# Latent attention: four of nine key tiles with one fp32 tile of exponentials and one plain fp32 value product

## The chip, the core and the metric

The kernel runs on one core of a Trainium2 chip. The core has a matrix engine (TensorE, PE in the profile, with its weight loads shown apart as PEld), a vector engine (VectorE, DVE), a scalar engine with the exponential (ScalarE, ACT), a general engine (GpSimd, POOL) and a sync engine that issues the DMAs (SyncE, SP). Each engine works through its own list of instructions in order and waits on semaphores for the others. The metric is the time of one execution on the device in microseconds; lower is better.

## The reference

Two layers of a diffusion trunk are computed in fp32 for 128 context tokens and 1024 latent tokens. Layer 0 joins a banded attention and a bidirectional state-space scan. Layer 1, which the change concerns, is a multi-head latent attention of 16 heads:

```python
def dense_attention(q, k, v, scale, sink=None):
    ...
    def one_block(qblk):
        s = jnp.einsum("bqhgd,bkhd->bhgqk", qblk, k).astype(jnp.float32) * scale
        ...
            p = jax.nn.softmax(s, axis=-1)
        return jnp.einsum("bhgqk,bkhd->bqhgd", p.astype(v.dtype), v)
...
    k = jnp.concatenate([k_lat, k_ctx], axis=1)
    v = jnp.concatenate([v_lat, v_ctx], axis=1)
    return mla_attend(q, k, v, g, w_out)
```

For every head the 1024 latent queries see 1024 latent keys and 128 keys of the cached context (nine key tiles of 128); the 128 new context tokens see only themselves (one key tile). Keys and queries have 96 columns, values 64.

## The kernel before

float32r is a type that the matrix engine reads at a reduced precision in one pass. To stay near fp32, the kernel splits nearly every operand into two float32r parts, high and low, whose sum is the fp32 value (`split`, L245: ACT rounds the high part, DVE or POOL subtracts for the low one), and multiplies three pairs of parts (`mm3`, L255). A few products run as plain fp32: the scan's state product (L992), the sums of the softmax (L1496) and some small ones.

Layer 1's attention is woven from generators. `head_main` (L1437) is the main stream. For each head it goes over three chunks of queries: 512 and 512 latent ones with nine key tiles each, and the 128 context ones with one. A step for one key tile does this:

- Three score products into one of two PSUM banks (L1449 to L1451). The row of minus the maximum is a 97th row of the operands, so that the exponential needs no further subtraction.
- Two exponentials from the same scores on ACT: `ph` as float32r (L1458) and `pf` as fp32 (L1459).
- One step later, in `rest`, DVE computes the low part `pl` = `pf` - `ph` (L1473) and POOL adds `pf` to the chunk's running denominators, `total` (L1477; L1475 for the single-tile chunk).
- Behind that, in `values`, two products with the values add into the chunk's bank `acco` (L1467 with `ph`, L1468 with `pl`). Their stationary operand is a tile of 128 keys by 128 columns: 64 columns with the high part of the values, 64 with the low part.

`gather` (L1484) adds both halves of the chunk's outputs (L1489, L1490), sums `total` over its partitions by a plain product with ones (L1496), and later divides and gates. The rings are short: three buffers for `pf` and `ph`, two for `pl`, two for `total`, two banks for scores.

Beside the main stream run the row maxima of the next heads (`head_max`: PE L1428, then a DVE reduction that the profile shows at L209, since its call is put off by `Steps.tick`), the projections of the next pair of heads (`operands`, with PE at L256 to L258 and splits at L249 and L250), and at the end the splitting of the output weights. `spread` (L1548) deals these evenly over the main steps. A scheduler of the tile framework then fixes the order on every engine from its own model of durations, so an edit in one place can move instructions of others.

Of the kernel before, what the change touches and what calls it, by code (L numbers as in the profile page):

```python
# [80 lines left out]
class Segment:  # L81
    """columns of one SBUF tile, handed out and taken back while the kernel is traced"""

# [26 lines left out]
class Memory:  # L110
    """four tiles of SBUF: R holds operands of float32r products, F everything else, S and G either by turns"""

# [25 lines left out]
class Space:  # L138
    """named rings of buffers in the memory"""

# [52 lines left out]
class Steps:  # L193
    """pieces of work put off by a number of steps of the stream that they go along with"""

# [25 lines left out]
def hybrid_trunk(ctx: ExitStack, tc: tile.TileContext, I, O, dbg=None, stage=99):  # L221
# [23 lines left out]
    def split(hi, lo, src, scale=None, lo_eng=None):  # L245
        """hi + lo == src * scale exactly; scale is None, a power of two or a [P, 1] operand."""
        lo_eng = lo_eng or dve
        if scale is None:
            act.copy(hi, src)  # L249
            lo_eng.tensor_tensor(lo, src, hi.bitcast(F32), ALU.subtract)  # L250
        else:
            act.activation(hi, src, AF.Copy if isinstance(scale, float) else AF.Identity, scale=scale)  # L252
            dve.scalar_tensor_tensor(lo, src, scale, hi.bitcast(F32), ALU.mult, ALU.subtract)
# [5 lines left out]

# [1 line left out]
    ident = const("ident", [128, 128], I["k_ident"])  # L261
# [8 lines left out]

# [1 line left out]
    gate_d = scratch("gate_d", [2, 2, D])  # L272
# [20 lines left out]

# [1 line left out]
    wp = Space(mem)  # L295
# [19 lines left out]

# [1 line left out]
    def condition():  # L317
# [25 lines left out]
    def modulation(sp, l, j, parts):  # L343
        """columns 256 j .. 256 j + 255 of the map of layer l; whole weights, or split ones where TensorE has no time to spare"""
        c0 = j * 256
# [42 lines left out]
    def rstd_of(p, ssq, n, width):  # L388
        """ssq [128, width] -> (ssq / n + eps) ** -0.5"""
        r = p.tile([128, width], F32, tag="rstd", name="rstd", bufs=4)  # L390
        pool.tensor_scalar(r, ssq, 1.0 / n, EPS, ALU.mult, ALU.add)
        pool.tensor_tensor(r, r, minus_half, ALU.pow)
        return r
# [7 lines left out]
    def weave(main, n_main, aux, n_aux):  # L401
        """n_aux steps of aux spread evenly over n_main steps of main"""
        done = 0
        for i, _ in enumerate(main):
            while done < n_aux and done * n_main < n_aux * (i + 1):
                next(aux, None)
                done += 1
        for _ in aux:
            pass

    def token_tile(hT, t):
        """the transposes of token tile t, by k: two parts"""
        c, o = divmod(t, CH // 128)
        return [h[:, :, o * 128:(o + 1) * 128] for h in hT[c]]
# [3 lines left out]

# [1 line left out]
    condition()  # L420
# [35 lines left out]

# [1 line left out]
    wp.drop("wr")  # L458
# [242 lines left out]

# [1 line left out]
    def fm_proj(w, b, hT, c):  # L703
        """128 columns of a slab for a chunk of tokens, columns by tokens"""
        acc = psum("mm", "acc")
        ws = slice(b * 128, (b + 1) * 128)
        for k in range(KT):
            mm3(acc[:, 0:CH], w[0][:, k, ws], w[1][:, k, ws], hT[c][0][:, k], hT[c][1][:, k], k == 0, k == KT - 1)
        return acc[:, 0:CH]
# [61 lines left out]
    def chunk_states(p, fb, xt, Bt):  # L771
        """states of two heads before every chunk, forward ones at rows 0..63, backward ones, counted from the last chunk, below"""
        g, h0 = slice(fb // 4 * 64, fb // 4 * 64 + 64), 2 * fb
# [146 lines left out]

# [1 line left out]
    mem.set("G", F32)  # L922
# [119 lines left out]

# [1 line left out]
    def norm_T(p, l, cond, xh, tok):  # L1044
        """modulated transpose of a normalised token tile"""
        for q in range(2):
# [9 lines left out]
    def residual(p, half, acc, x, gate, adder=pool):  # L1056
        """x[:, half] += gate * acc"""
        cs = slice(half * 512, (half + 1) * 512)
        tmp = p.tile([128, 512], F32, tag="rt", name="rt", bufs=2)
        dve.tensor_tensor(tmp, acc, gate[:, cs], ALU.mult)  # L1060
        adder.tensor_tensor(x[:, cs], x[:, cs], tmp, ALU.add)
# [90 lines left out]

# [1 line left out]
    mem.set("G", F32R)  # L1154
# [11 lines left out]
    with p6 as p:  # L1166
        order = [NLT] + list(range(NLT))

        def put_latent(tk, n):
            """tk [128, n * 128 + 96]: transposes of the columns of cq, ckv and (at rows 64..95) kpe"""  # L1170
            pt = psum("tr", "pt")
            for j in range(n):
                pe.transpose(pt[:, j * 128:(j + 1) * 128], tk[:, j * 128:(j + 1) * 128], ident)
            pe.transpose(pt[0:32, 384:512], tk[:, n * 128:n * 128 + 32], ident)
            return pt
# [71 lines left out]

# [1 line left out]
    uq = I["mla_w_uq"][0].rearrange("(k p) (h d) -> p k h d", p=128, d=96)  # L1249
# [20 lines left out]
    def pinned(f, *a):  # L1270
        """an instruction that stays behind those that its engine was given before"""
        tc.keep_in_program_order(f(*a))  # L1272
# [3 lines left out]
    def spare(name):  # L1276
        """a bank, to be read in the next step"""
        taken.append(steps.now)
        assert taken.count(steps.now) <= 4
        return psum(next(either), name)  # L1280
# [3 lines left out]
    def until(n):  # L1284
        """waits for the n-th step from now"""
        t = steps.now + n
# [48 lines left out]
    def quad_rope(Q):  # L1335
        """the rotated parts of four heads' queries"""
        qh, ql = quads[Q][0]
# [30 lines left out]
    def place(Q, pr, acc, dh, dl, cols):  # L1368
        """a pair of heads' rows of a projection into their operand sets"""
        for a in range(2):  # L1370
# [16 lines left out]
    def operands(pair):  # L1387
        """fills the operand sets of a pair of heads"""
        Q, pr = divmod(pair, 2)
# [10 lines left out]
    def head_max(h):  # L1400
        """row of -max of the scores, a group of query tiles at a time"""
        s = h % NSET
# [19 lines left out]
        for t0, n in ((0, 4), (4, 4), (NLT, 1)):  # L1422
            pm = p7.tile([128, 4, 3], F32, tag="pm", name="pm", bufs=3)
            spans = [(NL + 128, 128)] if t0 == NLT else [(c * CH, CH) for c in range(3)]
            for t in range(t0, t0 + n):
                for c, (k0, w) in enumerate(spans):
# [5 lines left out]
                    yield  # L1432

    CHUNKS = ((0, 512, range(9)), (512, 512, range(9)), (NL, 128, (9,)))
    behind = []

    def head_main(h, op, chunks=CHUNKS):  # L1437
        """a step per tile of keys: its scores and exponentials; the values of the tile before"""
        s, a = h % NSET, h % 2
        for q0, n, kts in chunks:  # L1440
# [5 lines left out]
            for i, kt in enumerate(kts):  # L1446
# [8 lines left out]
                pf = p7.tile([128, 512], F32, tag="pf", name="pf", bufs=3)[:, 0:n]  # L1455
                ph = p7.tile([128, 512], F32R, tag="ph", name="ph", bufs=3)[:, 0:n]
                pl = p7.tile([128, 512], F32R, tag="pl", name="pl", bufs=2)[:, 0:n]
                act.activation(ph, sc[:, 0:n], AF.Exp, scale=SCALE_M)  # L1458
                act.activation(pf, sc[:, 0:n], AF.Exp, scale=SCALE_M)  # L1459
# [3 lines left out]

                def values(V=quads[h // 4][2][h // 2 % 2][:, kt, a], ph=ph, pl=pl, acc=acc, total=total, i=i, last=i == len(kts) - 1, q0=q0, n=n):
                    if i == 0:
                        acc.append(psum("o", "acco")[:, 0:n])
                    pe.matmul(acc[0], V, ph, start=(i == 0), stop=False)  # L1467
                    pe.matmul(acc[0], V, pl, start=False, stop=last)  # L1468
                    if last:
                        after(1, gather, h, op, q0, n, acc[0], total)  # L1470

                def rest(pf=pf, ph=ph, pl=pl, total=total, i=i, alone=len(kts) == 1, first=first, values=values):
                    dve.tensor_tensor(pl, pf, ph.bitcast(F32), ALU.subtract)  # L1473
                    if alone:
# [9 lines left out]
    def gather(h, op, q0, n, acc, total):  # L1484
        """adds the two parts of a head's outputs; divides a pair of heads by the denominators, gates"""
        a, j = h % 2, h // 2
# [61 lines left out]
    def spread(n_main, *aux):  # L1548
        """called once a step of n_main: steps of every (generator, count) spread evenly"""
        done = [0] * len(aux)  # L1550
# [87 lines left out]

# [1 line left out]
    with p9 as p:  # L1640
# [59 lines left out]
```

## Time and profile before

| what | value |
|---|---|
| median of three runs | 1939.34 us (1937.37 to 1945.99) |
| span of the profiled execution | 1936.3 us |
| PE busy in it | 1770.5 us |
| DVE busy | 1338.3 us |
| ACT busy | 972.3 us |
| POOL busy | 849.1 us |
| granted TensorE clock, mean | 0.952 |
| from the first value product to the last sum of denominators | 1160 to 1836 us of the span |

The page gives no time of its own for the profiled execution beside its span; the median lies 3.0 us above it. Busy times are of single engines and overlap. In rows that group instructions, the part in front of the bar names line, engine, operation, output and inputs with their shapes and the count; behind it stand the busy time, the mean in ns of one, and the idle time in front with what ended it. A wait row names who waited, on whom, and total us, times and the longest. All SBUF tiles of this kernel are columns of four large tiles, so that names like arenaF say only which of the four; the line tells which work it is. A plain fp32 product appears as two instructions on PE.

### The profile page before, as it was taken

The page shows a single profiled execution, that of the slowest core. Times are in us where ns is not written, and L with a number is a line of the kernel's source. Part 1 is how long each engine was busy: PE and PEld are TensorE (multiplying, and loading weights), DVE is VectorE, ACT ScalarE, POOL GpSimd, SP SyncE. Part 2 cuts the span into 40 slices and gives each one's busy share as a digit, 9 for nine tenths or more (in the row PEclk, how much of TensorE's full clock was granted, in tenths as well). Part 3 has the DMA queues.
Part 4 walks back from the last instruction along what each step waited for, and adds up shares of the span by engine and source line. Part 5 has one row for each costly group of instructions (what it writes and reads, how often), then busy time and mean ns, then how long its engine had stood idle before and what let it go on. Part 6 is the DMA issues. An engine that isn't in the chain of part 4 may idle for free. (4 is left out here: it accounts for less than half of the span.)

```text
span 1936.3 us, 28171 instructions
## 1 busy us (share of the span) xinstructions
PE 1770.5 (91%) x9031; PEld 1405.9 (73%) x9031; DVE 1338.3 (69%) x2421; ACT 972.3 (50%) x2201; POOL 849.1 (44%) x781
## 2 busy tenths in 40 slices
PE   7899999999987898989999999998989899988898
PEld 3899999868766866767788986666666566654586
DVE  5666455654544577676654359999999899999833
ACT  5533224655654454444344236666567566765521
POOL 3410000233443346566340105866775586765632
PEclk9999999999988888989999989999989899998999
DMA  7333333343436786554535320211120121112352
GB/s 256 111 91 111 93 105 104 118 121 98 127 110 186 232 262 212 167 185 157 170 89 177 107 64 12 60 27 38 33 60 19 40 63 30 33 40 89 91 168 87
DMA packets 210664, 210.33 MB, mean 109 GB/s; under 512 B 36162, under 2 KB 175504, under 8 KB 210516
## 3 DMA queue, kind: packets, MB, share of 16 engines
q1 hardware_dynamic: 210372, 208.40, 35.7%
q8 instruction: 72, 1.18, 0.3%
q14 instruction: 76, 0.62, 0.1%
q0 software_dynamic: 144, 0.13, 0.0%
HBM read 151.94 MB, written 51.72 MB: 105 GB/s over the span
## 5 line engine op out<-in xcount | busy, mean ns | idle before, releaser
L1477 POOL TENSOR_TENSOR arenaF<-arenaF 128x512 f32<-128x512 f32 x256 | 390.9, 1528 | 171.4 <-PE den L1496 96.0
L256 PE MATMUL acc<-arenaR 128*128 128x384 f32 (+4 forms) x1152 | 390.6, 340 | 14.4 <-ACT arenaR L252 4.7
L257 PE MATMUL acc<-arenaR 128*128 128x384 f32 (+3 forms) x1080 | 362.7, 336 | 0.1
L258 PE MATMUL acc<-arenaR 128*128 128x384 f32 (+4 forms) x1056 | 352.1, 335 | 0.8 <-DVE arenaR L250 0.6
L256 PEld LDWEIGHTS acc<-arenaR 128*128 128x128 f32 x1152 | 224.3, 195 | 41.2 <-issue 7.0
L209 DVE TENSOR_REDUCE arenaF<-pp 128x1 f32<-128x384 f32 (+1 forms) x400 | 204.0, 534 | 21.6 <-PE pp L1428 18.9
L257 PEld LDWEIGHTS acc<-arenaR 128*128 128x128 f32 x1080 | 210.0, 194 | 10.7 <-issue 1.8
L258 PEld LDWEIGHTS acc<-arenaR 128*128 128x128 f32 x1056 | 206.0, 195 | 13.2 <-issue 3.0
L1473 DVE TENSOR_TENSOR arenaG<-arenaF,arenaS 128x512 fp32r<-128x512 f32 (+1 forms) x202 | 200.0, 996 | 3.9 <-PE acco L1468 2.7
L1459 ACT ACTIVATE arenaF<-sc 128x512 f32<-128x512 f32 (+1 forms) x304 | 174.3, 576 | 7.3 <-POOL arenaF L1477 6.7
L1468 PE MATMUL acco<-arenaG 128*128 128x512 f32 (+1 forms) x304 | 134.1, 444 | 42.9 <-DVE arenaG L1473 38.5
L1458 ACT ACTIVATE arenaS<-sc 128x512 fp32r<-128x512 f32 (+1 forms) x202 | 117.3, 582 | 91.0 <-PE sc L1451 46.1
L1005 ACT ACTIVATE arenaG<-arenaG,arenaF 128x128 f32<-128x128 f32 x288 | 88.4, 389 | 115.9 <-POOL arenaG L1003 115.4
L250 DVE TENSOR_TENSOR arenaR<-arenaF,arenaR 128x512 fp32r<-128x512 f32 (+2 forms) x135 | 115.3, 869 | 41.9 <-ACT arenaR L249 35.5
L249 ACT CAST arenaR<-arenaF 128x512 fp32r<-128x512 f32 (+3 forms) x151 | 91.6, 625 | 81.2 <-DMA arenaF<-in_ab_w_in_dram 19.1
L1468 PEld LDWEIGHTS acco<-arenaG 128*128 128x128 f32 x304 | 59.5, 196 | 98.7 <-DVE arenaG L1473 88.1
L258 PE MATMUL acc<-arenaR,arenaS 128*128 128x512 f32 (+1 forms) x336 | 128.9, 387 | 0.0
L749 POOL TENSOR_TENSOR arenaG<-arenaF,arenaG 128x512 fp32r<-128x512 f32 x28 | 48.6, 1734 | 151.4 <-PE acco L753 83.4
L1428 PE MATMUL pp<-arenaR 96*128 96x384 f32 x300 | 104.3, 385 | 8.4 <-DVE arenaF L209 4.2
L256 PE MATMUL acc<-arenaR,arenaS 128*128 128x512 f32 (+1 forms) x264 | 106.3, 403 | 1.0 <-ACT arenaS L249 0.7
L257 PE MATMUL acc<-arenaR,arenaS 128*128 128x512 f32 (+1 forms) x264 | 105.4, 399 | 0.0
L1449 PE MATMUL sc<-arenaR 96*128 96x512 f32 (+1 forms) x228 | 96.5, 423 | 7.1 <-ACT arenaF L1459 6.9
(339 smaller groups left out, 4052.9 us busy)
## 6 DMA issues: line engine op xcount, KB each, us to landing
arenaF<-in_ada_w_dram SPq DMA_DIRECT2D x96, 256.0 KB
arenaG<-cum_d SPq DMA_DIRECT2D x36, 512.0 KB
arenaF<-in_ab_w_in_dram SPq DMA_DIRECT2D x51, 256.0 KB
z_d<-arenaF SPq DMA_DIRECT2D x36, 128.0 KB
xs_d<-arenaF SPq DMA_DIRECT2D x8, 576.0 KB
arenaF<-xs_d SPq DMA_DIRECT2D x9, 512.0 KB
arenaF<-z_d SPq DMA_DIRECT2D x9, 512.0 KB
x_d<-arenaG SPq DMA_DIRECT2D x9, 512.0 KB
```

Source lines behind the costliest of these rows:

```text
L209: f()
L250: lo_eng.tensor_tensor(lo, src, hi.bitcast(F32), ALU.subtract)
L256: pe.matmul(out, ah, bh, start=first, stop=False)
L257: pe.matmul(out, ah, bl, start=False, stop=False)
L258: pe.matmul(out, al, bh, start=False, stop=last)
L1428: pe.matmul(pp[:, 0:w], AQ[s][0:96, t * 128:(t + 1) * 128], AK[s][0:96, k0:k0 + w], start=True, stop=True)
L1449: pe.matmul(sc[:, 0:n], AK[s][0:96, ks], BQ[s][:, qs], start=True, stop=False)
L1458: act.activation(ph, sc[:, 0:n], AF.Exp, scale=SCALE_M)
L1459: act.activation(pf, sc[:, 0:n], AF.Exp, scale=SCALE_M)
L1468: pe.matmul(acc[0], V, pl, start=False, stop=last)
L1473: dve.tensor_tensor(pl, pf, ph.bitcast(F32), ALU.subtract)
L1477: pool.tensor_tensor(total, first if i == 1 else total, pf, ALU.add)
```

## The change

Of the nine key tiles of a chunk, those with index 1, 3, 5 and 7, and the only tile of the context chunk, are called whole. For them `ph`, its exponential, `pl` and the subtraction are left out, and the values meet `pf` in one plain fp32 product; the stationary operand is the same tile, read as fp32. The other five key tiles stay as they were. Comments and docstrings are removed elsewhere in the file, and lines from L1434 on move down by one to eight.

```diff
+    WHOLE = 1, 3, 5, 7
...
-                ph = p7.tile([128, 512], F32R, tag="ph", name="ph", bufs=3)[:, 0:n]
-                pl = p7.tile([128, 512], F32R, tag="pl", name="pl", bufs=2)[:, 0:n]
-                act.activation(ph, sc[:, 0:n], AF.Exp, scale=SCALE_M)
+                whole = i in WHOLE or len(kts) == 1
+                ph = pl = None
+                if not whole:
+                    ph = p7.tile([128, 512], F32R, tag="ph", name="ph", bufs=3)[:, 0:n]
+                    pl = p7.tile([128, 512], F32R, tag="pl", name="pl", bufs=2)[:, 0:n]
+                    act.activation(ph, sc[:, 0:n], AF.Exp, scale=SCALE_M)
                 act.activation(pf, sc[:, 0:n], AF.Exp, scale=SCALE_M)
...
-                    pe.matmul(acc[0], V, ph, start=(i == 0), stop=False)
-                    pe.matmul(acc[0], V, pl, start=False, stop=last)
+                    if whole:
+                        pe.matmul(acc[0], V.bitcast(F32), pf, start=(i == 0), stop=last)
+                    else:
+                        pe.matmul(acc[0], V, ph, start=(i == 0), stop=False)
+                        pe.matmul(acc[0], V, pl, start=False, stop=last)
...
-                    dve.tensor_tensor(pl, pf, ph.bitcast(F32), ALU.subtract)
+                    if not whole:
+                        dve.tensor_tensor(pl, pf, ph.bitcast(F32), ALU.subtract)
```

In the kernel after, the scores are L1450 to L1452, the plain product L1472, the two parts L1474 and L1475, the subtraction L1481, the exponentials L1462 (`ph`) and L1463 (`pf`), the denominators' addition L1485 and their sum L1504.

PE's queue while the projections of the second pair of heads are made, from the last product of a key projection (L258) on. Before (a name in brackets is the semaphore for which the instruction waits):

```order
L258 MATMUL acc<-arenaR 128x256
L1449 MATMUL sc<-arenaR 128x512 [waits Activation_49]
L1450 MATMUL sc<-arenaR 128x512
L1451 MATMUL sc<-arenaR 128x512 [waits DMAHW2_49,DMAHW3_49,DMAHW1_49,DMAHW0_49]
L1428 MATMUL pp<-arenaR,arenaS 128x384 [waits DVE_49]
L1468 MATMUL acco<-arenaG 128x512 [waits DVE_49]
L1467 MATMUL acco<-arenaR,arenaG 128x512
L1449 MATMUL sc<-arenaR 128x512 [waits Activation_49]
```

The same place after:

```order
L258 MATMUL acc<-arenaR 128x256
L1475 MATMUL acco<-arenaG 128x512 [waits DVE_49]
L1472 MATMUL acco<-arenaF,arenaG 128x512
L1428 MATMUL pp<-arenaR,arenaS 128x384 [waits DVE_49,PE_49]
L1474 MATMUL acco<-arenaS,arenaG 128x512 [waits Activation_49]
L1428 MATMUL pp<-arenaR,arenaS 128x384 [waits DVE_49]
L1450 MATMUL sc<-arenaR 128x512 [waits Activation_49]
L1451 MATMUL sc<-arenaR 128x512
```

The plain product (L1472, its input `pf` in arenaF) stands directly behind the second part of the tile ahead of it (L1475), which waits for DVE, and the first part of the next tile (L1474) follows. That is so for 102 of the 144 plain products; before, the next tile's first part mostly stood in that place.

DVE's queue between the two splits of that key projection (L250, 64x256). Before:

```order
L250 TENSOR_TENSOR arenaR<-acc,arenaR 64x256 [waits Activation_49]
L209 TENSOR_REDUCE arenaF<-pp 128x1 [waits PE_49]
L1473 TENSOR_TENSOR arenaG<-arenaF,arenaS 128x512 [waits PE_49]
L209 TENSOR_REDUCE arenaF<-pp 128x1 [waits PE_49]
L1473 TENSOR_TENSOR arenaG<-arenaF,arenaS 128x512 [waits PE_49,Activation_49]
L250 TENSOR_TENSOR arenaR<-acc,arenaR 64x256 [waits Activation_49]
```

After, up to the next subtraction:

```order
L250 TENSOR_TENSOR arenaR<-acc,arenaR 64x256 [waits Activation_49]
L209 TENSOR_REDUCE arenaF<-pp 128x1 [waits PE_49] x2
L250 TENSOR_TENSOR arenaR<-acc,arenaR 64x256 [waits Activation_49]
L1407 TENSOR_REDUCE arenaF<-arenaF 128x4 [waits DVE_49]
L209 TENSOR_REDUCE arenaF<-pp 128x1 [waits PE_49]
L1408 TENSOR_SCALAR arenaF<-arenaF 128x4 [waits DVE_49]
L1481 TENSOR_TENSOR arenaG<-arenaF,arenaR 128x512 [waits Activation_49]
```

The two subtractions between the splits are gone, and the row maxima's reductions (L209) and the next ones' last steps (L1407, L1408) have moved up. POOL's queue keeps its additions, and SP's DMAs are nearly in the old order.

More of the change, by code (lines that the diff above doesn't have):

```diff
@@ L1462, in head_main, with values, rest @@
                     behind.pop()()
-                def values(V=quads[h // 4][2][h // 2 % 2][:, kt, a], ph=ph, pl=pl, acc=acc, total=total, i=i, last=i == len(kts) - 1, q0=q0, n=n):
+                def values(V=quads[h // 4][2][h // 2 % 2][:, kt, a], whole=whole, pf=pf, ph=ph, pl=pl, acc=acc, total=total, i=i, last=i == len(kts) - 1, q0=q0, n=n):
                     if i == 0:
                         acc.append(psum("o", "acco")[:, 0:n])
-                    pe.matmul(acc[0], V, ph, start=(i == 0), stop=False)
-                    pe.matmul(acc[0], V, pl, start=False, stop=last)
+                    if whole:
[3 more added lines that the diff above has]
+                        pe.matmul(acc[0], V, pl, start=False, stop=last)
                     if last:
                         after(1, gather, h, op, q0, n, acc[0], total)
-                def rest(pf=pf, ph=ph, pl=pl, total=total, i=i, alone=len(kts) == 1, first=first, values=values):
-                    dve.tensor_tensor(pl, pf, ph.bitcast(F32), ALU.subtract)
+                def rest(whole=whole, pf=pf, ph=ph, pl=pl, total=total, i=i, alone=len(kts) == 1, first=first, values=values):
+                    if not whole:
+                        dve.tensor_tensor(pl, pf, ph.bitcast(F32), ALU.subtract)
                     if alone:
```

## The prediction

> **What bounds the kernel now.** The first view is the table of stretches, cut where the attention's first value product starts and where its last denominator ends. Its columns are the stretch, its length, then busy time with the count of instructions for PE, PE's weight loads, DVE, ACT and POOL, then the granted clock, the DMA share and GB/s.
>
> ```profile
> 0.00:1160.00 1160.00, 1071.74 (x6184) 911.63 (x6185) 672.09 (x1289) 517.57 (x1243) 367.84 (x432) 0.95 0.47 144
> 1160.00:1836.00 676.00, 606.35 (x2444) 418.77 (x2444) 629.61 (x1093) 437.29 (x932) 449.61 (x313) 0.96 0.17 45
> 1836.00:1936.30 100.30, 92.44 (x405) 75.51 (x403) 36.56 (x40) 17.44 (x27) 31.69 (x36) 0.99 0.37 125
> ```
>
> The edited lines run only in the middle stretch of 676 us, and everything outside it stays. In it DVE is busy 630 us (93%), PE 606 us (90%), POOL 450 us (67%), ACT 437 us (65%). DMA is slight. PE's 90% flatters it, because each record contains the fill of the array. So the second view is the timeline of PE, to see how far apart matmuls start when nothing holds them: first a 512-wide float32r run, then a 384-wide one.
>
> ```profile
> 903.31 0.39 PE L256 MATMUL acc<-arenaR,arenaS 128*128 128x512 f32 x1
> 903.53 0.39 PE L257 MATMUL acc<-arenaR,arenaS 128*128 128x512 f32 x1
> 903.76 0.40 PE L258 MATMUL acc<-arenaR,arenaS 128*128 128x512 f32 x1
> ...
> 1207.56 0.34 PE L256 MATMUL acc<-arenaR 128*128 128x384 f32 x1
> 1207.74 0.34 PE L257 MATMUL acc<-arenaR 128*128 128x384 f32 x1
> ```
>
> A record lasts 0.39 us but the next starts after 0.22 to 0.24 us (I use 0.233, the middle of many such steps), and after 0.18 us at 384 columns. How much PE really has to do follows from the counts in the same stretch, one row for each output tile, here sc (scores), acco (values), pp (row maxima), acc (projections), den (denominators) and pt (transposes):
>
> ```profile
> 1160.00:1836.00 676.00, 270.57 (x906) 169.94 (x906) 318.82 (x606) 0.96 0.17 45
> 1160.00:1836.00 676.00, 207.28 (x608) 108.33 (x608) 25.55 (x47) 22.89 (x48) 0.96 0.17 45
> 1160.00:1836.00 676.00, 128.94 (x377) 72.58 (x377) 192.14 (x377) 0.96 0.17 45
> 1160.00:1836.00 676.00, 88.70 (x411) 71.36 (x410) 73.55 (x161) 56.51 (x143) 0.96 0.17 45
> 1160.00:1836.00 676.00, 39.92 (x95) 4.56 (x96) 21.38 (x47) 0.96 0.17 45
> 1160.00:1836.00 676.00, 14.10 (x47) 4.16 (x47) 0.00 (x0) 11.47 (x47) 0.96 0.17 45
> ```
>
> Scores and values: 858 + 576 wide ones by 0.233 = 334 us. pp: 361 by 0.18 = 65. acc: 411 of mixed width, about 0.175 each by the two steps above, 72. den: 32 wide by 0.95 and 16 narrow by 0.31 (rows below), 35. The 128-wide rest and the transposes, an estimate, 11. That is **517 us of real PE work**, so 159 us of the stage are PE waiting, loading weights in the open, or running at a lowered clock. The third view, the table of waits for this stretch, says on whom (us in total, times, longest):
>
> ```profile
> PEld acco L1468 <- DVE arenaG L1473: 88.1, 116, 2.5
> PE acco L1468 <- DVE arenaG L1473: 38.5, 65, 1.9
> PEld pp L1428 <- DVE arenaF L209: 22.8, 63, 1.4
> PEld sc L1449 <- ACT arenaF L1459: 20.0, 38, 1.4
> PEld den L1496 <- issue: 14.0, 41, 0.7
> PEld pp L1428 <- issue: 8.5, 19, 1.6
> PE sc L1449 <- ACT arenaF L1459: 7.6, 15, 1.2
> PEld pt L1413 <- DVE arenaF L1408: 7.5, 12, 3.0
> ```
>
> 126.6 of these 207 us (61%) are the value product waiting for DVE's subtraction at L1473. So DVE is the bound today, and it is exactly DVE that the change relieves; but PE, which the change loads, has only those 159 us to give.
>
> **The change part by part.** Four of nine key tiles in each of 32 chunks are 128 wide tiles; the 16 context chunks are 16 narrow ones. The groups by shape give what goes:
>
> ```profile
> L1473 DVE TENSOR_TENSOR arenaG<-arenaF,arenaS 128x512 fp32r<-128x512 f32 x192 | 197.1, 1032 | 3.9 <-PE acco L1468 2.7 <-ACT arenaF L1459 1.1
> L1473 DVE TENSOR_TENSOR arenaG<-arenaF,arenaR 128x512 fp32r<-128x512 f32 x96 | 98.4, 1025 | 1.8 <-PE acco L1468 1.4 <-ACT arenaF L1459 0.2
> L1458 ACT ACTIVATE arenaS<-sc 128x512 fp32r<-128x512 f32 x192 | 114.5, 598 | 88.1 <-PE sc L1451 44.7 <-DVE arenaG L1473 29.9 <-PE acco L1467 4.1
> ```
>
> DVE loses 128 x 1.03 = 132 us and about 5 us of narrow ones: 630 becomes 493 us, 73% of today's stage. ACT loses 128 x 0.598 = 77 us and about 4: 437 becomes 356 us, 53%. POOL's sums stay, 450 us. None of this is a gain by itself; it counts only as far as PE stops waiting.
>
> What PE gains: the plain product of a 128x128 stationary with 512 columns. The nearest rows of before are the plain fp32 products of the scan stage (64 rows, but also 128 stationary columns and 512 moving ones), and the denominators (one stationary column):
>
> ```profile
> 912.23 1.12 PE L992 MATMUL off<-arenaG,arenaF 64*128 64x512 f32 x2
> 913.28 0.50 PE L256 MATMUL acc<-arenaR 128*128 128x512 f32 x1
> 913.62 0.40 PE L257 MATMUL acc<-arenaR 128*128 128x512 f32 x1
> ...
> 918.62 0.39 PE L258 MATMUL acc<-arenaR 128*128 128x512 f32 x1
> 918.94 1.12 PE L992 MATMUL off<-arenaG,arenaF 64*128 64x512 f32 x2
> ...
> 1206.06 0.34 PE L258 MATMUL acc<-arenaR,arenaS 128*128 128x384 f32 x1
> 1206.33 1.02 PE L1496 MATMUL den<-arenaF 128*1 128x512 f32 x2
> 1207.27 0.45 PE L1428 MATMUL pp<-arenaR 96*128 96x384 f32 x1
> ...
> 1208.72 0.38 PE L1496 MATMUL den<-arenaF 128*1 128x128 f32 x2
> 1209.03 0.45 PE L1428 MATMUL pp<-arenaR 96*128 96x384 f32 x1
> ```
>
> One plain product is two records (x2). From its start to the next it takes 1.05 us (912.23 to 913.28), 0.94 us with a single stationary column. It starts 0.32 instead of 0.23 us behind its forerunner (918.62 to 918.94), and its follower's successor comes 0.34 instead of 0.23 us later (913.28 to 913.62). Together 1.05 + 0.09 + 0.11 = 1.25 us against 2 x 0.233 = 0.466 for the two parts: **+0.78 us a tile, 100 us for 128**. The low end is the denominators' 0.94 + 0.09 + 0.11 = 1.14 (+86 us); I take 1.25, since the stationary has 128 columns. A narrow one costs 0.31 + 0.2 against some 0.16: 16 x 0.35 = 6 us. PE's work becomes 517 + 106 = **623 us**.
>
> The Trainium skill, TensorE: Matmul & The Clock Gate, section "Step-by-step: what each phase is for", says that the next weights load while this matmul runs; FP8 and Floating Point Precision, section "TensorE Precision Notes", counts four passes for true fp32. By both a plain tile would take 4 x 0.233 = 0.93 us and the 128 tiles add 59 us, 41 us less than my sum. The trace agrees with the four passes and disagrees with the hiding: at each change between fp32 and float32r the rows above show about 0.1 us, and 0.1 more between the two records. I go by the rows.
>
> What is left of the 159 us decides. DVE's part is 61% of it, 97 us: 4/9 of those waits vanish, since a plain tile needs no subtraction, and the others shrink with DVE at 73%; I take a quarter, 25 us. The other 62 us (a lowered clock is some 27 of them, 0.04 x 676; the rest are waits for ACT and for reductions, and loads around the denominators) I take at half, 30 us, because ACT and DVE both have slack then. Stage: 623 + 55 = 678 us, 2 us over today. Bounds: at best only edges remain, 22 us, stage 645 (-31); at worst only 4/9 of 126.6 goes, 103 us remain, stage 726 (+50).
>
> Two edits have no direct price. The fp32 tile pf now stays in use until PE has read it, and its ring has three buffers; today's rows for such waits are small:
>
> ```profile
> ACT arenaF L1459 <- POOL arenaF L1477: 6.7, 14, 1.0
> ACT arenaS L1458 <- PE acco L1467: 4.6, 8, 1.2
> ```
>
> I take nothing, up to 10 us, covered by two steps between the exponential and the slot's reuse. The new order of PE's queue puts the plain product mostly right behind its neighbour's second part, which waits for DVE; behind it stand the next scores, for which ACT waits. That is the second rival.
>
> **The rivals.**
>
> *Faster: PE is kept fed.* PE reaches 95% of real work once DVE has slack, and its lowered clock goes with the gaps that cause it. For it speaks how the clock falls:
>
> ```profile
> 1408.00:1412.00 4.00, 2.35 (x7) 1.15 (x7) 2.66 (x10) 2.18 (x7) 3.58 (x3) 0.90 0.49 135
> 1412.00:1416.00 4.00, 4.00 (x13) 3.21 (x13) 2.00 (x4) 1.57 (x6) 3.03 (x3) 0.50 0.58 161
> ```
>
> PE busy for 2.35 of 4 us, then a granted clock of 0.50. If such gaps close, most of the 27 us return, 35 us of the 159 remain, the stage takes 658 us and the kernel 1936.3 - 18 + 3 = 1921 us. Against it: the stage would have PE with work for 95% of the time, in order, with two score banks. The Trainium skill's section "The HAM clock gate" in TensorE: Matmul & The Clock Gate states that an idle window of some 3.4 us halves the clock; these two rows agree in kind.
>
> *Slower: PE's queue is held.* PE is the bound and its in-order queue still stops at the second parts; the 1.25 us products then stand between a late subtraction and the scores, ACT runs dry, and every wait is now a wait of the bound. With 85 us remaining the stage takes 708 us, the kernel 1971 us. It decides from 53 us of remaining waits on (676 - 623). For it: 102 of the 144 plain products stand directly behind a second part in the new order. Against it: DVE at 73% should have finished that part earlier.
>
> That the change doesn't take effect has no chance: the order has 144 plain products and the subtractions fewer by as many.
>
> **How the numbers follow.** The span of the profiled execution is 1936.3 us; the median of the three runs, 1939.34, is 3.0 above, and I carry that over. Forecast: +2 us, **1941 us**, chance 0.36 for all within 0.5% (about what a measurement of this kernel can tell from no change), that is 43 to 63 us of remaining waits. The faster rival has 0.34, the slower one 0.30. The range reaches from the best bound, 1908 us, to near the worst, 1978 us; the forecast's own is 1930 to 1949 us.
>
> **What would show it.** Plain products start-to-start near 1.05 us with about 0.1 us on either side (0.93 without would make it 40 us faster). L1473's group at 160 instructions, DVE near 500 us, ACT near 356 us in the stage. The waits of PE for that line under 40 us if the forecast or the faster rival holds, over 60 if the slower one does. PE's chain share should grow at DVE's cost. The granted clock at 0.99 speaks for the faster rival. I am wrong outright if POOL, or waits for its sums, becomes the bound.

## The result, and the profile after

The changed kernel takes 1892.67 us (median of four runs, 1888.87 to 1893.89) against 1938.36 us before; the ratio is 0.9752, 95% interval 0.9732 to 0.9773. That is 2.5% faster. The forecast was 1941 us with a range from 1908 to 1978 us, so the measured time lies below the range. The span of the profiled execution fell from 1936.3 to 1887.1 us. The same cut as before, from the attention's first value product to its last denominator (columns: stretch, length, busy time and count of PE, weight loads, DVE, ACT and POOL, then clock, DMA share, GB/s):

```profile
1157.00:1786.00 629.00, 599.25 (x2441) 417.65 (x2439) 497.41 (x950) 370.67 (x788) 428.89 (x313) 0.98 0.19 49
```

The stage went from 676 to 629 us, 47 of the 49 us. DVE's busy time came out as forecast (497 us; 493 was forecast), ACT's fell somewhat less (371 us; 356 forecast): two exponentials in a row overlap (in this trace one starts at 1295.99 and lasts 0.60 us, the next starts at 1296.49), so leaving one out saves about 0.50 us and not the 0.598 us of its record. The groups of the changed lines, as far as the page prints them:

```profile
L1481 DVE TENSOR_TENSOR arenaG<-arenaF,arenaS 128x512 fp32r<-128x512 f32 x106 | 99.1, 935 | 30.7 <-ACT arenaF L1463 29.4
...
L1462 ACT ACTIVATE arenaS<-sc 128x512 fp32r<-128x512 f32 x106 | 63.4, 598 | 55.6 <-PE sc L1452 54.6
```

and the table of waits of the stage, with the rows that answer to those of before:

```profile
PEld sc L1450 <- issue: 19.1, 80, 0.2
PEld pp L1428 <- DVE arenaF L209: 17.4, 31, 1.0
...
PEld sc L1450 <- ACT arenaF L1463: 8.1, 12, 2.5
...
PEld acco L1475 <- DVE arenaG L1481: 7.4, 17, 0.9
PEld acco L1472 <- ACT arenaF L1463: 7.3, 8, 2.0
```

PE's load unit used to wait 88.1 us for the subtraction; it waits 7.4 us now. DVE hardly ever stood idle in front of a subtraction before (3.9 us for 192 of them); now it does for 30.7 us in front of 106, nearly all of it for ACT's fp32 exponential. ACT, in front of its float32r exponential, used to wait for PE's scores (44.7 of 88.1 us) and for DVE (29.9 us); now 54.6 of 55.6 us are for the scores. So DVE now waits for ACT, and ACT for PE: the roles have turned round. How PE runs a plain product when its inputs are ready shows in its timeline (start, duration, line; x2 is two records merged):

```profile
1295.80 0.40 PE L1475 MATMUL acco<-arenaG 128*128 128x512 f32 x1
1296.03 1.02 PE L1472 MATMUL acco<-arenaF,arenaG 128*128 128x512 f32 x2
1296.49 0.80 PE L1450 MATMUL sc<-arenaS,arenaR 96*128 96x512 f32 x1
1297.12 0.40 PE L1451 MATMUL sc<-arenaS,arenaR 96*128 96x512 f32 x1
```

The record of the next score starts early, at 1296.49, and lasts 0.80 us because it stands behind the second half of the plain product. So one has to read on to the record after it: from 1296.03 to 1297.12 run one plain product and one score product of 0.233 us. That leaves **0.86 us for the plain product**, gaps included; there is none ahead (1295.80 to 1296.03 is the usual step). Over all 128 wide ones the median is 0.86 us. I had taken 1.25.

### The profile page after: what moved, and what is told of

Its sections match the earlier page's. It is cut to its first block, busy times and chain, and to the rows that moved or that the text cites. A ratio compares the mean times of both kernels' runs of the same rounds, so it can differ in the third digit from the quotient of the medians.

```text
span 1887.1 us, 27621 instructions
## 1 busy us (share of the span) xinstructions
PE 1758.9 (93%) x9031; PEld 1400.0 (74%) x9031; DVE 1208.2 (64%) x2277; ACT 905.3 (48%) x2057; POOL 823.9 (44%) x781
## 5 line engine op out<-in xcount | busy, mean ns | idle before, releaser
L1485 POOL TENSOR_TENSOR arenaF<-arenaF 128x512 f32<-128x512 f32 x256 | 378.3, 1478 | 185.8 <-ACT arenaF L1463 102.3
L258 PE MATMUL acc<-arenaR 128*128 128x384 f32 (+4 forms) x1056 | 350.4, 333 | 0.2
L209 DVE TENSOR_REDUCE arenaF<-pp 128x1 f32<-128x384 f32 (+1 forms) x400 | 203.9, 538 | 37.5 <-PE pp L1428 34.7
L258 PEld LDWEIGHTS acc<-arenaR 128*128 128x128 f32 x1056 | 204.4, 194 | 11.9 <-issue 2.7
L1463 ACT ACTIVATE arenaF<-sc 128x512 f32<-128x512 f32 (+1 forms) x304 | 171.8, 579 | 62.2 <-POOL arenaF L1485 27.6
L250 DVE TENSOR_TENSOR arenaR<-arenaF,arenaR 128x512 fp32r<-128x512 f32 (+2 forms) x135 | 116.4, 877 | 43.8 <-ACT arenaR L249 39.3
L1472 PE MATMUL acco<-arenaF,arenaG 128*128 128x512 f32 (+1 forms) x288 | 139.8, 567 | 4.2 <-ACT arenaF L1463 4.2
L258 PE MATMUL acc<-arenaR,arenaS 128*128 128x512 f32 (+1 forms) x336 | 128.2, 385 | 0.0
L1481 DVE TENSOR_TENSOR arenaG<-arenaF,arenaS 128x512 fp32r<-128x512 f32 x106 | 99.1, 935 | 30.7 <-ACT arenaF L1463 29.4
L1450 PE MATMUL sc<-arenaR 96*128 96x512 f32 (+1 forms) x228 | 113.7, 499 | 4.4 <-ACT arenaF L1463 4.3
L1428 PE MATMUL pp<-arenaR 96*128 96x384 f32 x300 | 98.8, 379 | 13.0 <-DVE arenaS L250 9.1
L1452 PE MATMUL sc<-arenaR 97*128 97x512 f32 (+1 forms) x228 | 90.0, 398 | 0.0
L1462 ACT ACTIVATE arenaS<-sc 128x512 fp32r<-128x512 f32 x106 | 63.4, 598 | 55.6 <-PE sc L1452 54.6
```

The source lines that it names most:

```text
L209: f()
L258: pe.matmul(out, al, bh, start=False, stop=last)
L1428: pe.matmul(pp[:, 0:w], AQ[s][0:96, t * 128:(t + 1) * 128], AK[s][0:96, k0:k0 + w], start=True, stop=True)
L1450: pe.matmul(sc[:, 0:n], AK[s][0:96, ks], BQ[s][:, qs], start=True, stop=False)
L1472: pe.matmul(acc[0], V.bitcast(F32), pf, start=(i == 0), stop=last)
L1485: pool.tensor_tensor(total, first if i == 1 else total, pf, ALU.add)
```

## The experiments

Two questions were open: whether that price explains the whole miss, and why the same kind of product costs 0.86 us here and 1.25 us (L992) or 1.15 us (L1496) elsewhere in the same kernel. All are edits of the changed kernel. The stretches of the table further down are cut like those above. The kernel before, run beside them, had medians from 1940.91 to 1943.7 us.

**A full stationary for the denominators.**

```diff
-    ones = p7.tile([128, 1], F32, name="ones")
+    ones = p7.tile([128, 128], F32, name="ones")
...
-            pe.matmul(den[0:1, 0:n], ones, total, start=True, stop=True)
+            pe.matmul(den[:, 0:n], ones, total, start=True, stop=True)
```

> The changed kernel, but the sum of the denominators (L1504) uses a 128-column stationary of ones instead of one column; the output rows beyond the first are not read. In the changed kernel this sum costs PE 1.14 to 1.23 us in all (0.95 from its start to the next, the rest as gaps of about 0.1 us on both sides), the plain value product, which has 128 rows and 128 columns, only 0.86 us without gaps. Theory (the weights of a full 128x128 stationary load behind the running product, those of a smaller one do not): the sum falls to about 0.86 us, PE saves 32 x 0.3 = 10 us and some 3 on the narrow ones, and since PE is now the bound the kernel takes 1880 to 1890 us. Rival (the gaps come from waiting for two semaphores, for which the record shows separate wait instructions on PE's load queue at L1504 and L992 and none at L1472): the sum stays at 1.15 to 1.2 us and the time at 1893 us.

Measured: 1887.2 us (median of five), ratio to before 0.9724 (0.9693 to 0.9756). The sum's whole cost, gaps on both sides included, fell from a median of 1.19 us to 0.86 us, over the 23 wide sums of each kernel that stand between products of 384 or 512 columns. The records of the waits that the rival blamed stayed: lines of L1504 in the changed kernel, then in this one (first the weight loads, then the separate waits):

```profile
L1504 PEld LDWEIGHTS den<-arenaF x96: 79/82/84, 1185.6 to 1786.1; 128*1 128x1 f32 x96
...
L1504 PEldq EVENT_SEMAPHORE  x41: 51/51/51, 1184.4 to 1718.7; - x41
```

```profile
L1504 PEld LDWEIGHTS den<-arenaF x96: 186/189/193, 1199.1 to 1793.1; 128*128 128x128 f32 x96
...
L1504 PEldq EVENT_SEMAPHORE  x41: 51/51/51, 1199.1 to 1725.5; - x41
```

41 waits in both, a weight load more than twice as long (189 against 82 ns), and yet the product is cheaper. The rival with the semaphores falls.

**Half a stationary for the values.** The low parts of the values are left out for the four key tiles.

```diff
-                        pe.matmul(acc[0], V.bitcast(F32), pf, start=(i == 0), stop=last)
+                        cols = 64 if n == 512 else 128
+                        pe.matmul(acc[0][0:cols], V[:, 0:cols].bitcast(F32), pf, start=(i == 0), stop=last)
```

> The changed kernel, but the plain value products of the 512-wide chunks use 64 stationary columns, so the low parts of the values are left out for the four key tiles. Theory of the full stationary: each of the 128 products shows the gaps of about 0.1 us and costs 1.15 to 1.25 us instead of 0.86, PE gets 37 to 50 us more work, the kernel takes 1915 to 1940 us. Rival (semaphores): 0.86 us and 1893 us as before.

Measured: 1923.63 us (one run). PE's timeline of this kernel, which has the plain product at L1473:

```profile
1211.94 0.39 PE L1476 MATMUL acco<-arenaG 128*128 128x512 f32 x1
1212.27 1.07 PE L1473 MATMUL acco<-arenaF,arenaG 128*64 128x512 f32 x2
1213.27 0.50 PE L1450 MATMUL sc<-arenaR 96*128 96x512 f32 x1
1213.60 0.39 PE L1451 MATMUL sc<-arenaR 96*128 96x512 f32 x1
```

and PE's weight loads at the same place, then at the place quoted above in the changed kernel:

```profile
1211.78 0.19 PEld L1476 LDWEIGHTS acco<-arenaG 128*128 128x128 f32 x1
1212.26 0.19 PEld L1473 LDWEIGHTS acco<-arenaF,arenaG 128*64 128x64 f32 x2 [0.30 <-issue]
1213.27 0.19 PEld L1450 LDWEIGHTS sc<-arenaR 96*128 96x128 f32 x1 [0.81 <-issue]
```

```profile
1295.57 0.19 PEld L1475 LDWEIGHTS acco<-arenaG 128*128 128x128 f32 x1
1295.80 0.42 PEld L1472 LDWEIGHTS acco<-arenaF,arenaG 128*128 128x128 f32 x2
1296.46 0.19 PEld L1450 LDWEIGHTS sc<-arenaS,arenaR 96*128 96x128 f32 x1 [0.24 <-issue]
```

With 64 columns the load begins at 1212.26, 0.32 us after the start of the product before, whose step of 0.23 us is over by then, and the gaps are back: 0.10 us ahead (0.33 instead of 0.23 from L1476), 1.00 us to the next start, 0.10 us behind. Together 1.20 us. With 128 columns the load begins at 1295.80, together with the product before, and nothing shows. Fewer columns made the product dearer by a third of a microsecond. The stage of this kernel takes 661 us, against 629 with the full stationary:

```profile
1160.00:1821.00 661.00, 641.12 (x2440) 386.66 (x2440) 503.26 (x950) 371.25 (x788) 427.02 (x313) 0.98 0.18 46
```

**PE's added work alone, and DVE's relief alone.** In the first, the float32r exponential and the subtraction are made for all tiles and their results are not read for the four; in the second, the four tiles use the float32r exponential in both products, so the low part of their exponentials is left out and no subtraction is made.

```diff
-                if not whole:
+                if True:
                     ph = p7.tile([128, 512], F32R, tag="ph", name="ph", bufs=3)[:, 0:n]
...
-                    if not whole:
+                    if True:
                         dve.tensor_tensor(pl, pf, ph.bitcast(F32), ALU.subtract)
```

> The changed kernel, but the float32r exponential and the subtraction are still made for the four key tiles (nobody reads their results); the values meet the fp32 tile in a plain product. So only PE's added work is left. Theory (DVE's subtractions bounded the kernel; the plain products cost PE 0.39 us each): DVE stays at some 630 us in the stage, PE's added 50 us fall mostly into its waits: 1935 to 1960 us. Rival (the gain came from the order of PE's queue, with fewer and longer products, not from DVE): below 1915 us.

```diff
                     if whole:
-                        pe.matmul(acc[0], V.bitcast(F32), pf, start=(i == 0), stop=last)
+                        pe.matmul(acc[0], V, ph, start=(i == 0), stop=False)
+                        pe.matmul(acc[0], V, ph, start=False, stop=last)
```

> The changed kernel, but the four key tiles keep the float32r exponential and use it in both value products; no subtraction and no plain product (the low part of their exponentials is left out). So only DVE's relief is left. Theory: PE's work is 517 us again, with 50 to 80 us of waits the stage takes 570 to 600 us, the kernel 1830 to 1865 us. Rival (PE's waits follow from scores, banks and ACT, not DVE): 1890 us or more.

Measured, one run each: 1941.77 us with PE's added work alone, no change against 1940.91 us beside it; 1862.37 us with DVE's relief alone, 78 us less. The change as a whole brings 46 us. So the added products cost nothing while DVE bounds the stage, and once DVE is out of the way the whole change stands some 30 us above DVE's relief alone. These 30 us hold the 50 us of added products against what ACT's shorter work gives back; no run here has ACT's relief by itself. The rows of the stage, PE alone first:

```profile
1159.00:1839.00 680.00, 630.12 (x2443) 414.12 (x2442) 630.92 (x1093) 431.41 (x932) 446.09 (x313) 0.97 0.17 44
...
1164.00:1760.00 596.00, 556.43 (x2444) 414.81 (x2443) 501.13 (x951) 431.69 (x931) 425.26 (x314) 0.98 0.20 51
```

DVE is busy 631 of 680 us in the first and 501 of 596 us in the second; ACT's time is the same in both. That a different order on PE brought the gain is not borne out: the first run has the plain products in much the same order (102 of 144 right behind a second part, as in the changed kernel), and gains nothing.

**How many tiles.** Each takes the kernel of the first experiment, with another set of key tiles made plain:

```diff
-    WHOLE = 1, 3, 5, 7
+    WHOLE = 3, 7
```

> The kernel of e1 (128-column sum of the denominators) with only key tiles 3 and 7 of nine as plain products. Theory (each tile made plain adds 0.39 us to PE and takes 1.03 us from DVE; 32 chunks): against e1 PE loses 25 us and DVE gains 66 us (to about 565 us in the stage, 87% of some 650 us). DVE is nearly the bound again: stage 635 to 655 us, kernel 1895 to 1920 us. Rival (only PE's work counts once DVE has any slack): below 1880 us.

> The kernel of e1 with key tiles 1, 4 and 7 as plain products. PE loses 12.5 us, DVE gains 33 us. Theory: both engines at about 85% to 90% of the stage, near the flat minimum: 1880 to 1900 us.

> The kernel of e1 with key tiles 1, 2, 4, 5, 7 and 8 as plain products. PE gains 25 us (to about 590 us of real work), DVE loses 66 us. Theory: PE is the bound, few of its waits are left to take: stage 625 to 645 us, kernel 1885 to 1905 us. Rival (DVE still bounds at four tiles): below 1875 us.

> The kernel of e1 with all nine key tiles as plain products: no subtraction and no second exponential is left. PE has 62 us more work than with four (some 627 us), DVE loses 165 us. Theory: PE is the only bound, its waits fall to 25 to 45 us: stage 650 to 672 us, kernel 1910 to 1935 us. Rival (a plain product costs 1.25 us, as I had predicted): stage above 740 us, kernel above 2000 us.

Measured, one run each: two tiles 1889.15 us, three 1885.39, six 1904.26, nine 1900.87. The stage for two, three, four (the first experiment), six and nine:

```profile
1163.00:1786.00 623.00, 577.28 (x2446) 427.52 (x2444) 554.36 (x1013) 400.44 (x853) 435.44 (x313) 0.98 0.19 49
...
1161.00:1782.00 621.00, 586.21 (x2437) 429.23 (x2437) 540.58 (x980) 382.36 (x819) 430.50 (x313) 0.98 0.18 48
...
1171.00:1793.00 622.00, 589.88 (x2440) 429.20 (x2439) 499.90 (x950) 369.62 (x786) 431.14 (x313) 0.98 0.19 49
...
1168.00:1802.00 634.00, 613.30 (x2442) 433.27 (x2441) 436.48 (x886) 342.81 (x724) 402.51 (x313) 0.98 0.17 48
...
1159.00:1798.00 639.00, 633.78 (x2443) 429.34 (x2442) 348.57 (x790) 298.40 (x629) 375.02 (x313) 0.99 0.17 48
```

Read with PE's real work, counted as in the prediction (517 us, plus 32 x 0.39 = 12.5 us for each tile made plain, plus 2 us for the narrow chunks, less 4 us for the wider sum: the prediction counts a sum from its start to the next, 0.95 us wide and 0.31 us narrow, and these become 0.86 and 0.22 us; the gaps around the old sum are in what is left over). Each stage is that of one profiled execution; the times of two, three, six and nine tiles are single ones:

| plain tiles of nine | stage, us | PE's real work | left over | DVE busy | kernel, us |
|---|---|---|---|---|---|
| 0 (before) | 676 | 517 | 159 | 630 | 1938.36 |
| 2, wide sum | 623 | 540 | 83 | 554 | 1889.15 |
| 3, wide sum | 621 | 553 | 68 | 541 | 1885.39 |
| 4 (the change) | 629 | 569 | 60 | 497 | 1892.67 |
| 4, wide sum | 622 | 565 | 57 | 500 | 1887.2 |
| 6, wide sum | 634 | 590 | 44 | 436 | 1904.26 |
| 9, wide sum | 639 | 628 | 11 | 349 | 1900.87 |

With nine, PE has work for 628 of 639 us, and the others wait for it: the rows of that kernel's waits begin with

```profile
ACT arenaF L1463 <- PE sc L1452: 181.9, 203, 3.4
POOL arenaF L1485 <- ACT arenaF L1463: 146.4, 150, 18.4
DVE arenaF L209 <- PE pp L1428: 140.3, 127, 2.9
```

Two of the four expectations missed. With two tiles I expected 635 to 655 us for the stage, since DVE would be nearly the bound; it is busy 554 of 623 us. PE's two units do wait 61 us for the subtraction again (39.5 and 21.7; with the change 7.4 and 1.5), but PE has 25 us less work than with the change and the wide sum, so the stage stays as short. With nine I expected 25 to 45 us to remain, and it was 11. The rival with 1.25 us a product, over 740 us, is far off. The two single times from six tiles on are not quite in order, because the stretch ahead of the stage, whose instructions are the same, ended at 1168 us in the run with six and at 1159 us in the one with nine; the stages are in order.

**The two best, timed together.** The kernel with three plain tiles and the wide sum, and beside it the changed kernel itself.

> The kernel of e6 again, timed: three plain key tiles and the 128-column sum. Theory (flat minimum between two and four tiles, the wider sum saves some 10 us of PE work): 1882 to 1888 us, 3 to 9 us below the changed kernel timed beside it. Rival (no difference beyond the spread): within 2 us of it.

> The changed kernel itself, timed beside e9 on the same chip. Every theory: 1888 to 1895 us.

Measured: 1886.56 us (median of six), ratio to before 0.9714 (0.9681 to 0.9748); the changed kernel beside it 1893.39 us, 0.9742 (0.9705 to 0.9778). It is 6.8 us lower, as expected, but the intervals overlap, so that a gain over the changed kernel is likely and not settled.

## Why the prediction was wrong

- *DVE is the bound today, and the change relieves it.* Right. With DVE's relief alone the kernel is 78 us faster; with PE's work alone it is unchanged.
- *What DVE loses.* Right: 497 us of the stage, 493 forecast.
- *What is left of PE's 159 us.* Right within 5 us in the total, which is partly luck. I forecast 55 us; with the measured price PE's work is 517 + 128 x 0.39 + 2 = 569 us, and 629 - 569 = 60 us remain. But I had 25 us of them as waits for the subtraction, and these went from 126.6 us on both units to 9 us; the rest, which I had at 30 us, is then some 50 us. The two misses cancel. The split rested on the 126.6 us being 61% of eight rows of waits; all rows of the two units in that stretch add up to 263.5 us, of which they are 48%.
- *The price of the plain product.* **This step failed.** I took 1.25 us, +0.78 us a tile and 100 us in all, from the products of L992, and 1.14 us as the low end. Measured is 0.86 us, +0.39 us a tile, 50 us in all. With that price, 2 us for the narrow ones and my own 55 us of waits, my sum gives a stage of 624 us, where I wrote 678 and 629 was measured: the two prices make 54 us, and the kernel would have come out at 1887 us. The experiment with half a stationary is nearly the kernel that I had forecast, with 1.20 us a product: by my sum its stage would take 668 us, and it took 661. The mechanism was the forecast one, that PE becomes the tighter engine; the term that was mis-sized is this one.
- *Why it was off.* L992 has 64 rows in its stationary, L1496 one column. I put their gaps down to the change between fp32 and float32r, and the new product makes the same change without a gap (L1475 to L1472 at 1296.03). The row that I called nearest differed from the new product in what matters: experiments one and two move the price in both directions (1.19 to 0.86 us when the sum's stationary is made full, 0.86 to 1.20 us when the values' is halved). For the 64 rows of L992 no experiment was made. I bounded the price by two rows that shared the same defect, so the bounds did not hold it.
- *The rule that I set aside.* The Trainium skill (TensorE: Matmul & The Clock Gate, "Step-by-step: what each phase is for") says that the next weights load while this matmul runs. The trace after agrees for a 128x128 stationary: the load at 1295.80 starts with the product before. The rows of before disagreed for smaller ones in plain fp32 (the load of L992 at 918.94 starts 0.32 us behind the product before it, at 918.62), and they still do. With that page and the four passes the sum would have been 41 us lower, 1900 us.
- *The faster rival* was right in its sign and in the clock (0.98 in the stage, 0.96 before), but for another reason than the one I gave it: 60 us of waits remained, not 35.
- *The slower rival* had the new order hold PE's queue. The table of waits shows 7.4 us for it.
- *One sign failed.* PE's share of the chain that ended last was to grow at DVE's cost. DVE's fell from 11% to 1% of the span, but PE's fell too, from 10% to 7%.

## What to carry to other kernels

When a new operation has no row of its own, the nearest row is the one that agrees in type and in the shape of both operands; a row that differs in one of them is not a bound, and one small run of the operation itself is worth more than two such rows. Sum what the engine that is to take the work really has to do, by start-to-start steps, before counting the relief of another: here it told the total of the waits to 5 us, though not its parts. Moving work from a full engine to the next one pays only up to the point where both are equally full, and the minimum is flat there (two to four tiles of nine within 2 us of the stage).

## What the runs showed of the hardware

In these runs a plain fp32 product with 512 columns costs PE 1.25 us with a 64x128 stationary (the rows of the prediction), 1.20 us with 128x64, 1.14 to 1.23 us with 128x1 and 0.86 us with 128x128, in a stream of float32r products whose step is 0.233 us. The difference goes with the weight load, which starts ahead only in the last case. The size of the stationary doesn't decide this alone. A float32r product of layer 0 (L752, the low parts of its values) has a 128x64 stationary too, and its load starts with the product before and no gap shows; from the changed kernel:

```profile
324.80 0.39 PE L751 MATMUL acco<-arenaG 128*65 128x512 f32 x1
324.81 0.13 PEld L752 LDWEIGHTS acco<-arenaG 128*64 128x64 f32 x1
325.03 0.40 PE L752 MATMUL acco<-arenaG 128*64 128x512 f32 x1
```

So the late load goes with a small stationary in plain fp32; why, stays open. Whether 96 rows would count as full in plain fp32, as they do for the float32r scores, wasn't tried. The trace shows the 0.86 us as two records. Counted as the four passes of the prediction they are 0.215 us each; the Trainium skill gives 512 / 2.4 + 2.5 = 216 ns from one isolated matmul of 512 columns to the next at the full clock (TensorE: Matmul & The Clock Gate, "Back-to-back issue gap"), and by this count the products of these runs, in their stream, agree with it, while the float32r steps of 0.233 us are a little longer.
